# Pool inputs kept in PSUM, head sums through DRAM, token sums in groups of four: a hybrid decoder step on one core

## The chip, the core and the metric

The kernel runs on one core of a Trainium2 chip. Its engines are TensorE (PE, with its weight loads shown as PEld), VectorE (DVE), ScalarE (ACT), GpSimd (POOL) and SyncE (SP), which issues the DMAs. The metric is the device time of one execution in microseconds, the median of several runs.

## The reference

Two trunk layers of a decoder step over 576 tokens: 512 of a prompt and 8 sequences of 8 new tokens. Each layer, cut to what matters:

```python
h = rmsnorm(x, pre_g)
u, gp, q, k, v, gr = split(h @ w_in)             # 2048 -> 6 x 1024
pool_y = pool_mixer(u, ...) * silu(gp)           # window means less u, 4 groups of 256, times w_pool
ret_y = head_rmsnorm(retention(q, k, v, S0)) * silu(gr)   # 4 heads of 256
mix = concat(pool_y, ret_y) @ w_out
x = x + rmsnorm(mix, post_g)
ple = rmsnorm(p @ w_ple, ple_g)                  # 256 -> 2048
gate = sigmoid(x @ w_ple_gate + b_ple_gate)
x = x + gate * ple
```

The windows of the four pool groups are 2, 4, 8 and 16. The outputs are the tokens, the new retention states and the last 15 pool inputs of each sequence.

## The kernel before

Activations stand with channels on the 128 partitions and the 576 tokens in the free dimension, in tiles of 128 x 576 that are worked in two halves of 288 (HN). Every float32 product is made of three passes over rounded parts: `split` rounds a tensor on ScalarE (L90) and takes the rest on VectorE (L91), weights included (`split_part`, four tiles of 128 x 128 at a time).

The input projection's inner dimension of 2048 is cut in two. The first half goes through a Strassen-like scheme (`unit`, L116 to L118) and its results are stored to DRAM (`proj_dram`). The second half runs later, when the result is needed: `columns(pr)` yields the two output tiles of a pair. For each it loads the first half's result into a tile `t` of tag `part` (L478), calls `gemm` (16 channels' weights, 48 matmuls of 128 x 288, L136, into two accumulators of tag `acc`), and adds the two (L484). An accumulator is a PSUM bank; there are four of tag `acc`, two of `pb`, two of `po`.

A layer runs in this order: `in_first` (the first halves), `in_phase` (four heads, `head(0..3)`, then the pool groups 3, 2, 1, 0 with `pool_group(g)`), `out_phase` (the output projection in units, its norm, the embedding, the gate projection).

`head(h)` ends with a norm over its 256 channels (`rsqrt`, with `token_sums` at L292 and a broadcast at L310), the product with its silu gate (L653) and two stores into `m_dram[l][8 + 2h + i]`. Its state update (L354 to L377) streams 8 states through four buffers.

`pool_group(g)` loads the group's weights and state (`u` buffers, L660 and L662), and for both columns makes `e`, a tile of tag `d` with 15 zeros ahead of the prompt tokens (L668, L669), and the sample tokens behind the state in `es` (L670). GpSimd makes the window sums by doubling (L681, L682, in tiles of tag `tmp` and `es`), VectorE the mean less the input (L685 to L690). Two small gemms with the pool weights follow (L699, accumulators `po`), then the gate and scale into `y`, again of tag `d` (L703), and a store.

After each pool group, `operands(mix_loader(l, 8), [j], out_ops, tag="part")` prepares a quarter of the output projection's inputs: it loads two head outputs (tag `x`) and splits them, takes four sums and differences of their halves (`sums_of_blocks`, L194 to L197, into two tiles of tag `part`) and splits those.

In the embedding (L761 to L773) each of 16 output tiles is a gemm of 12 matmuls; ScalarE squares the two accumulators (L316, into a tile of tag `u`) and copies them (L771), TensorE adds the squares over the channels with a matrix of ones, 32 columns wide, one quarter of the tokens to each quarter of the partitions (L292, shown as two instructions per quarter), and the tile is stored.

Buffers belong to tags with a fixed count: `part` 4, `x` 4, `d` 4, `tmp` 4, `u` 6, `g` 2, `es` 2, `raw` 2 (1 MB each), `wh` and `wl` 5. The order on each engine and queue is made by a planner from the program order, the dependences and the free buffers, with costs of its own; `issue_after` and the added dependences of `after_all` constrain it by hand.

Of the kernel before, what the change touches and what calls it, by code (L numbers as in the profile page):

```python
# [38 lines left out]
def decoder_kernel(ctx: ExitStack, tc: tile.TileContext, a, decay8):  # L39
# [44 lines left out]
    ple_dram = [dram(f"ple{l}") for l in range(L)]  # L84
    gate_dram = [dram(f"gate{l}") for l in range(L)]
    proj_dram = [dram(f"proj{l}", 48) for l in range(L)]

# [40 lines left out]

    def gemm(w, xs, new=acc_tile, by_half=False):
        acc = [new()[:, :HN] for _ in range(2)]  # L130
        n = len(w)
        for hs in ((0,), (1,)) if by_half else ((0, 1),):
            for i, ((wh, wl), (xh, xl)) in enumerate(zip(w, xs)):
                for passno, (u, v) in enumerate(((wh, xh), (wh, xl), (wl, xh))):
                    for h in hs:
                        nc.tensor.matmul(  # L136
                            acc[h], u, v[:, h * HN:(h + 1) * HN],
                            start=(i == 0 and passno == 0), stop=(i == n - 1 and passno == 2),
                        )
        return acc  # L140
# [44 lines left out]

    def sums_of_blocks(ops, pairs=range(4), tag="u", engines=None):
        for j in pairs:
            x1, x2, new = ops["src"][j]
            b11, b12 = x1[:, :HN], x1[:, HN:]
            b21, b22 = x2[:, :HN], x2[:, HN:]  # L190
            eng = engines[j] if engines else nc.vector
            t12, t34 = (buf(tag) for _ in range(2))
            with order(ops):
                eng.tensor_tensor(out=t12[:, :HN], in0=b12, in1=b11, op=ALU.subtract)  # L194
                eng.tensor_tensor(out=t12[:, HN:], in0=b22, in1=t12[:, :HN], op=ALU.subtract)
                eng.tensor_tensor(out=t34[:, :HN], in0=b22, in1=b12, op=ALU.subtract)
                last = eng.tensor_tensor(out=t34[:, HN:], in0=b21, in1=t12[:, HN:], op=ALU.subtract)  # L197
            if eng is nc.vector:
                ops["tail"] = last
# [7 lines left out]
    def operands(xs, pairs=range(4), ops=None, tag="u", slots=own_slots):  # L207
        ops = operand_set() if ops is None else ops
        for j in pairs:
            blocks(xs, [j], ops, slots)  # L210
            sums_of_blocks(ops, [j], tag)
        return ops
# [77 lines left out]
    def token_sums(sums, src, start, stop):  # L290
        for q in range(4):
            nc.tensor.matmul(sums[32 * q:32 * q + 32], ones, src[:, q * QN:(q + 1) * QN], start=start, stop=stop)  # L292

    def rsqrt(out, srcs, n, sums=None):
        if sums is None:
# [11 lines left out]
        for h in range(2):  # L307
# [3 lines left out]
            nc.scalar.copy(half(out, h), rows)  # L311

    def square(out, src):
        if isinstance(src, list):
            for h in range(2):
                nc.scalar.activation(half(out, h), src[h], AF.Square)  # L316
        else:
            nc.scalar.activation(out, src, AF.Square)
# [12 lines left out]
    def load_tables():  # L331
# [8 lines left out]
        consts["invcnt"] = load_const("invcnt", [P, 4, 16])  # L340

    def after_all(ins, others):
        for other in others:
            tc.add_manual_dep(
                ins.ins, other.ins.name, mybir.DependencyInfo(mybir.DependencyClass.Sync, mybir.DependencyReason.DATA),
                reason="one burst",
            )

# [120 lines left out]
    def in_phase(l, raws, r2, rB, cos, sin):  # L469
        b_ring, st_ring, rot_ring, s0_ring = Ring(0, 12), Ring(12, 4), Ring(16, 8), Ring(24, 4)  # L470

        def columns(pr):
            keys = [("in2", p) for p in pairs] + [("out", 0, 0), ("out", 0, 1)]
            i = keys.index(("in2", pr))
            raw = raws.pop(("in2", pr))
            for c in range(2):
                t = buf("part")
                nc.sync.dma_start(out=t, in_=proj_dram[l][2 * pr + c])  # L478
                w = split_weights(raw, 8 * c, 8)
                if c == 1:  # L480
                    fetch(l, raws, keys[i + 1:i + 3])
                acc = gemm(w, r2)
                for h in range(2):
                    nc.vector.tensor_tensor(out=half(t, h), in0=acc[h], in1=half(t, h), op=ALU.add)  # L484
                yield t
# [74 lines left out]
        def head(h):  # L560
# [91 lines left out]
            for i, g in enumerate(silu_gates(20 + h)):  # L652
                nc.vector.tensor_tensor(out=o[i], in0=o[i], in1=g, op=ALU.mult)  # L653
                nc.sync.dma_start(out=m_dram[l][8 + 2 * h + i], in_=o[i])

        def pool_group(g):
# [8 lines left out]
            xs = []  # L665
            for i, t in enumerate(columns(g)):
                e = buf("d", (P, BUF + NP))
                nc.vector.memset(e[:, :BUF], 0.0)  # L668
                nc.vector.tensor_tensor(out=e[:, BUF:], in0=t[:, :NP], in1=rB[:, :NP], op=ALU.mult)  # L669
                nc.vector.tensor_tensor(  # L670
                    out=es[:, i, :, BUF:], in0=t[:, NP:].rearrange("p (b s) -> p b s", s=NS),
                    in1=rB[:, NP:].rearrange("p (b s) -> p b s", s=NS), op=ALU.mult,
# [39 lines left out]
        for j, g in enumerate(groups):  # L712
            pool_group(g)
            operands(mix_loader(l, 8), [j], out_ops, tag="part")
        return out_ops

    def mix_loader(l, first):
        def xs(k):
            t = buf("x")
            nc.sync.dma_start(out=t, in_=m_dram[l][first + k])  # L720
            return t
        return xs

    def out_phase(l, raws, ops_out):
# [5 lines left out]
        def out_step(n, g, p):  # L730
# [7 lines left out]
            if g == 0 and 1 <= p < 5:  # L738
                j = p - 1
                with order(ops[0]):  # L740
                    operands(mix_loader(l, 0), [j], ops[1], tag="d", slots=spare_slots if j < 2 else early_slots)
            if g:
# [12 lines left out]
        for k in range(2):  # L755
# [4 lines left out]
            pp.append((hi, lo))  # L760
        sums = mix_tile()[:, :QN]  # L761
        for c8 in range(2):
            raw = load_weights(a["w_ple"][l, :, c8 * 8:(c8 + 1) * 8].rearrange("p c k n -> p (c k) n"))
            w = split_weights(raw, 0, 16)
            for c in range(8):
                ct = c8 * 8 + c
                acc = gemm(w[2 * c:2 * c + 2], pp)
                t, sq = buf("part"), buf("u")
                square(sq, acc)
                for i in range(2):  # L770
                    nc.scalar.copy(half(t, i), acc[i])  # L771
                token_sums(sums, sq, ct == 0, ct == KT - 1)
                nc.sync.dma_start(out=ple_dram[l][ct], in_=t)  # L773

        def residual(first):
# [193 lines left out]
```

## Time and profile before

| | |
|---|---|
| median of 3 runs | 2217.16 us (2216.82 to 2217.84) |
| the profiled execution | 2217.77 us, span 2216.0 us |
| TensorE busy | 2185.6 us, 99% |
| weight loads busy | 2143.3 us, 97% |
| VectorE busy | 1733.7 us, 78% |
| ScalarE busy | 1057.0 us, 48% |
| GpSimd busy | 174.5 us, 8% |
| granted TensorE clock, mean | 0.996 |
| DMA | 361.99 MB, mean 163 GB/s |

The span reaches from the first to the last instruction. Matmuls overlap, so a busy TensorE is not one at its peak: where its stream is unbroken, one matmul of 128 x 288 follows another every 130 ns or so, while each is shown as 290 to 300 ns long.

### The profile page before, as it was taken

Reading aid. Unit: us, or ns where it says so; the run is one execution under the profiler, and the core shown is the slowest. Engines: PE = TensorE matmul, PEld = TensorE weight load, DVE = VectorE, ACT = ScalarE, POOL = GpSimd, SP = SyncE. Lnnn points to the kernel's source line nnn. Section 1 sums busy time; section 2 is a strip of 40 time slices with the busy share of each in tenths; the row PEclk is TensorE's granted clock in tenths of the full one; section 3 lists DMA queues with packets and bytes.
Section 4 is the critical chain, followed back from the end, with each engine's and each line's share of the span. In section 5 each row is a group of like instructions: output and inputs, shape, how many; then the busy total and the mean of one; then the engine's idle time right before and its main releaser. Section 6 shows DMA issues by size and latency. Waiting matters only on the chain.

```text
span 2216.0 us, 42622 instructions
## 1 busy us (share of the span) xinstructions
PE 2185.6 (99%) x16692; PEld 2143.3 (97%) x16692; DVE 1733.7 (78%) x3146; ACT 1057.0 (48%) x2097; POOL 174.5 (8%) x145
## 2 busy tenths in 40 slices
PE   8999999999999999999999999999999999999998
PEld 8999999999999999899999999999999899998998
DVE  8788766667689998788977886666676899988865
ACT  5465433444334555655545554434443345566532
POOL 2000000000043110000020000000002411100000
PEclk9999999999999999999999999999999999999999
DMA  6455455546443333556644444455555443345554
GB/s 222 149 195 165 155 168 165 169 157 191 154 159 129 133 128 122 196 176 208 216 157 149 169 156 152 160 177 173 164 164 165 155 135 130 106 149 192 176 194 156
DMA packets 137706, 361.99 MB, mean 163 GB/s; under 512 B 14496, under 2 KB 51872, under 8 KB 116640
## 3 DMA queue, kind: packets, MB, share of 16 engines
q1 hardware_dynamic: 137504, 359.26, 49.1%
q8 instruction: 131, 2.15, 0.4%
q14 instruction: 71, 0.58, 0.1%
HBM read 273.17 MB, written 86.04 MB: 162 GB/s over the span
## 4 chain that ended last, share of the span: by engine, by line
PE 87%; DVE 7%; DMA 4%; issue 2%; ACT 0%; SPq 0%; POOL 0%; DVEq 0%; ACTq 0%
PE acc L136 30%; PE acc L118 13%; PE acc L116 13%; PE acc L117 13%; PE acc L226 4%; PE pb L117 3%; PE pb L116 3%; PE pb L118 3%; DMA x<-ple 2%; DVE wl L91 1%; PE po L292 1%; PE po L359 1%; PE pb L375 1%; PE po L136 1%; PE pb L549 1%
## 5 line engine op out<-in xcount | busy, mean ns | idle before, releaser
L136 PE MATMUL acc<-m,wh 128*128 128x288 f32 x3584 | 661.1, 298 | 11.0 <-DVE part L484 11.0
L90 ACT CAST wh<-raw 128x512 fp32r<-128x512 f32 x567 | 350.5, 619 | 506.2 <-PE acc L136 260.7
L117 PE MATMUL acc<-m,wh 128*128 128x288 f32 x1944 | 572.8, 296 | 0.0
L116 PE MATMUL acc<-m,wh 128*128 128x288 f32 x1944 | 571.2, 295 | 0.5 <-ACT m L249 0.5
L118 PE MATMUL acc<-m,wl 128*128 128x288 f32 x1944 | 566.7, 295 | 0.7 <-DVE wl L91 0.7
L136 PEld LDWEIGHTS acc<-m,wh 128*128 128x128 f32 x3584 | 537.9, 190 | 19.1 <-issue 18.0
L91 DVE TENSOR_TENSOR wl<-raw,wh 128x512 fp32r<-128x512 f32 x567 | 407.2, 719 | 134.8 <-ACT wh L90 124.9
L136 PE MATMUL acc<-m,wl 128*128 128x288 f32 x1792 | 399.2, 296 | 0.0
L116 PEld LDWEIGHTS acc<-m,wh 128*128 128x128 f32 x1944 | 364.6, 188 | 1.9 <-ACT m L249 1.0
L117 PEld LDWEIGHTS acc<-m,wh 128*128 128x128 f32 x1944 | 364.9, 188 | 0.0
L118 PEld LDWEIGHTS acc<-m,wl 128*128 128x128 f32 x1944 | 362.4, 188 | 1.4 <-DVE wl L91 1.4
L90 ACT CAST wh<-S 128x512 fp32r<-128x512 f32 x356 | 220.4, 620 | 252.9 <-PE acc L117 139.7
L136 PEld LDWEIGHTS acc<-m,wl 128*128 128x128 f32 x1792 | 294.6, 190 | 1.9 <-issue 1.3
L91 DVE TENSOR_TENSOR wl<-S,wh 128x512 fp32r<-128x512 f32 x356 | 250.5, 705 | 22.0 <-ACT wh L90 20.5
L484 DVE TENSOR_TENSOR part<-acc,part 128x288 f32<-128x288 f32 x192 | 79.3, 449 | 62.4 <-PE acc L136 57.5
L239 POOL TENSOR_TENSOR S<-raw 128x512 f32<-128x512 f32 x45 | 70.3, 1562 | 713.6 <-DVE wl L91 352.6
L239 DVE TENSOR_TENSOR S<-raw 128x512 f32<-128x512 f32 x133 | 93.3, 701 | 8.5 <-DMA raw<-in_w_in 7.0
L682 POOL TENSOR_TENSOR es<-u 128x176 f32<-128x176 f32 x16 | 14.9, 937 | 1055.5 <-DVE u L670 1053.7
L117 PE MATMUL pb<-m,wh 128*128 128x288 f32 x324 | 95.5, 295 | 0.0
L116 PE MATMUL pb<-m,wh 128*128 128x288 f32 x324 | 95.1, 294 | 0.0
L118 PE MATMUL pb<-m,wl 128*128 128x288 f32 x324 | 95.1, 293 | 0.0
L249 ACT COPY d<-acc 128x288 f32<-128x288 f32 x228 | 86.1, 394 | 0.0
(265 smaller groups left out, 3412.1 us busy)
## 6 DMA issues: line engine op xcount, KB each, us to landing
raw<-in_w_in SPq DMA_DIRECT2D x95, 1024.0 KB, 5.3
raw<-in_w_out SPq DMA_DIRECT2D x32, 1024.0 KB, 4.9
raw<-in_w_gate SPq DMA_DIRECT2D x32, 1024.0 KB, 5.3
proj<-d SPq DMA_DIRECT2D x96, 288.0 KB, 2.1
part<-proj SPq DMA_DIRECT2D x96, 288.0 KB, 3.0
m<-in_state_ret SPq DMA_DIRECT2D x64, 256.0 KB, 3.1
out_new_ret_s<-m SPq DMA_DIRECT2D x64, 256.0 KB, 3.4
x<-m SPq DMA_DIRECT2D x48, 288.0 KB, 3.1
```

Of the source, the lines that this page charges most:

```text
L90: nc.scalar.copy(hi, src)
L91: return nc.vector.tensor_tensor(out=lo, in0=src, in1=hi.bitcast(F32), op=ALU.subtract)
L116: nc.tensor.matmul(out, wh, xh, start=start, stop=False, **kw)
L117: nc.tensor.matmul(out, wh, xl, start=False, stop=False, **kw)
L118: nc.tensor.matmul(out, wl, xh, start=False, stop=stop, **kw)
L136: nc.tensor.matmul(acc[h], u, v[:, h * HN:(h + 1) * HN], start=(i == 0 and passno == 0), stop=(i == n - 1 and passno == 2),)
L226: nc.tensor.matmul(acc[h], w[:, j], xs[h][passno == 1], start=(i == 0 and j == 0 and passno == 0), stop=(i == 1 and j == 3 and passno == 2),)
L239: eng.tensor_tensor(out=s, in0=x, in1=y, op=op)
L249: ops["tail_act"] = nc.scalar.copy(dst, src)
L292: nc.tensor.matmul(sums[32 * q:32 * q + 32], ones, src[:, q * QN:(q + 1) * QN], start=start, stop=stop)
L359: mm = nc.tensor.matmul(po_s[32 * r:32 * r + 32, bg], qrep[:, dt, b * 32:b * 32 + 32], s0s[r][:, dt], start=(dt == 0), stop=(dt == 1),)
L484: nc.vector.tensor_tensor(out=half(t, h), in0=acc[h], in1=half(t, h), op=ALU.add)
```

## The change

Three edits.

1. *Pool columns.* In `columns(pr, seeded=True)`, used by `pool_group` alone, the loaded tile `t` is copied by ScalarE into the two accumulators ahead of the gemm, whose matmuls then all accumulate (`seed`). The adds of L484 fall away there; the accumulators themselves are yielded, and the products of L669 (now two, one per half) and L670 read PSUM.
2. *Head sums.* The four sums and differences that `sums_of_blocks` takes of two head outputs are taken at the end of `head`, into two tiles of tag `x`, and stored (`sums_dram`). After a pool group they are loaded (tag `x`) instead of computed (tag `part`).
3. *Embedding squares.* The squares go to buffers of tags `tmp` (4), `g` (2) and `u` (2), and their token sums are issued four tiles at a time; the first matmul of such a burst is made to wait for the last square.

The core of the diff (`loader(tiles)` takes the place of `mix_loader(l, first)` and reads any list of DRAM tiles; `after_all` moves up unchanged):

```diff
+    sums_dram = [dram(f"sums{l}", 8) for l in range(L)]
...
-    def gemm(w, xs, new=acc_tile, by_half=False):
+    def gemm(w, xs, new=acc_tile, by_half=False, seed=None):
         acc = [new()[:, :HN] for _ in range(2)]
         n = len(w)
+        if seed is not None:
+            for h in range(2):
+                nc.scalar.copy(acc[h], half(seed, h))
...
-                            start=(i == 0 and passno == 0), stop=(i == n - 1 and passno == 2),
+                            start=(seed is None and i == 0 and passno == 0), stop=(i == n - 1 and passno == 2),
+                            skip_group_check=seed is not None,
...
+    def block_sums(eng, x1, x2, t12, t34):
+        b11, b12 = x1[:, :HN], x1[:, HN:]
+        b21, b22 = x2[:, :HN], x2[:, HN:]
+        eng.tensor_tensor(out=t12[:, :HN], in0=b12, in1=b11, op=ALU.subtract)
+        eng.tensor_tensor(out=t12[:, HN:], in0=b22, in1=t12[:, :HN], op=ALU.subtract)
+        eng.tensor_tensor(out=t34[:, :HN], in0=b22, in1=b12, op=ALU.subtract)
+        return eng.tensor_tensor(out=t34[:, HN:], in0=b21, in1=t12[:, HN:], op=ALU.subtract)
+
+    def sums_of_blocks(ops, pairs=range(4), tag="u", engines=None, sums=None):
         for j in pairs:
             x1, x2, new = ops["src"][j]
             eng = engines[j] if engines else nc.vector
+            if sums:
+                t12, t34 = sums(2 * j), sums(2 * j + 1)
+            else:
+                t12, t34 = (buf(tag) for _ in range(2))
+                with order(ops):
+                    last = block_sums(eng, x1, x2, t12, t34)
+                if eng is nc.vector:
+                    ops["tail"] = last
...
+    def together(sums, srcs, start, stop):
+        for i, src in enumerate(srcs):
+            for q in range(4):
+                mm = nc.tensor.matmul(
+                    sums[32 * q:32 * q + 32], ones, src[:, q * QN:(q + 1) * QN],
+                    start=start and i == 0, stop=stop and i == len(srcs) - 1,
+                )
+                if q == i == 0:
+                    after_all(mm, [last_square[0]])
...
-                nc.scalar.activation(half(out, h), src[h], AF.Square)
+                last_square[0] = nc.scalar.activation(half(out, h), src[h], AF.Square)
...
-        def columns(pr):
+        def columns(pr, seeded=False):
...
+                if seeded:
+                    yield gemm(w, r2, seed=t)
+                    continue
                 acc = gemm(w, r2)
...
+            sums = [buf("x") for _ in range(2)]
+            block_sums(nc.vector, *o, *sums)
+            for i, t in enumerate(sums):
+                nc.sync.dma_start(out=sums_dram[l][2 * h + i], in_=t)
...
-            for i, t in enumerate(columns(g)):
+            for i, acc in enumerate(columns(g, seeded=True)):
                 e = buf("d", (P, BUF + NP))
                 nc.vector.memset(e[:, :BUF], 0.0)
-                nc.vector.tensor_tensor(out=e[:, BUF:], in0=t[:, :NP], in1=rB[:, :NP], op=ALU.mult)
+                nc.vector.tensor_tensor(out=e[:, BUF:BUF + HN], in0=acc[0], in1=rB[:, :HN], op=ALU.mult)
+                nc.vector.tensor_tensor(out=e[:, BUF + HN:], in0=acc[1][:, :NP - HN], in1=rB[:, HN:NP], op=ALU.mult)
                 nc.vector.tensor_tensor(
-                    out=es[:, i, :, BUF:], in0=t[:, NP:].rearrange("p (b s) -> p b s", s=NS),
+                    out=es[:, i, :, BUF:], in0=acc[1][:, NP - HN:].rearrange("p (b s) -> p b s", s=NS),
                     in1=rB[:, NP:].rearrange("p (b s) -> p b s", s=NS), op=ALU.mult,
                 )
...
             pool_group(g)
-            operands(mix_loader(l, 8), [j], out_ops, tag="part")
+            operands(loader(m_dram[l][8:]), [j], out_ops, sums=loader(sums_dram[l]))
...
+        squares = []
         for c8 in range(2):
...
-                t, sq = buf("part"), buf("u")
+                t, sq = buf("part"), buf(("tmp", "tmp", "tmp", "tmp", "g", "g", "u", "u")[ct % 8])
                 square(sq, acc)
                 for i in range(2):
                     nc.scalar.copy(half(t, i), acc[i])
-                token_sums(sums, sq, ct == 0, ct == KT - 1)
                 nc.sync.dma_start(out=ple_dram[l][ct], in_=t)
+                squares.append(sq)
+                if len(squares) == 4:
+                    together(sums, squares, ct == 3, ct == KT - 1)
+                    squares = []
```

## Rows read from the trace of the kernel before

**Rows 1.** The page: TensorE's own line (busy time, share of the span, instructions) and the engines' shares of the chain that ended last.

```profile
PE 2185.6 (99%) x16692; PEld 2143.3 (97%) x16692; DVE 1733.7 (78%) x3146; ACT 1057.0 (48%) x2097; POOL 174.5 (8%) x145
...
PE 87%; DVE 7%; DMA 4%; issue 2%; ACT 0%; SPq 0%; POOL 0%; DVEq 0%; ACTq 0%
```

**Rows 2.** The waits of TensorE, longest first in total: who waited, for whom, us in total, times, longest.

```profile
PE acc L136 <- DVE part L484: 11.0, 4, 3.0
```

**Rows 3.** Windows around the waits of rows 2, TensorE alone. Columns: stretch in us, its length, TensorE busy (matmuls), granted clock, DMA share, GB/s.

```profile
640.00:643.00 3.00, 0.07 (x1) 0.83 0.97 303
643.00:646.00 3.00, 2.92 (x12) 0.50 0.97 368
646.00:649.00 3.00, 3.00 (x15) 0.53 0.87 307
...
1741.00:1744.00 3.00, 3.00 (x13) 0.52 0.86 310
...
1774.00:1777.00 3.00, 3.00 (x18) 0.71 0.28 65
1777.00:1780.00 3.00, 3.00 (x19) 0.73 0.95 383
```

**Rows 4.** The time order of VectorE in the pool stage of layer 0: start in us, length in us, instruction; in brackets the idle time before it and who ended it.

```profile
570.26 0.81 DVE L484 TENSOR_TENSOR part<-acc,part 128x288 f32<-128x288 f32 x2
...
576.77 0.82 DVE L484 TENSOR_TENSOR part<-acc,part 128x288 f32<-128x288 f32 x2 [2.01 <-PE acc L136]
...
585.97 0.35 DVE L670 TENSOR_TENSOR u<-part,long 128x64 f32<-128x64 f32 x2
...
600.09 0.81 DVE L484 TENSOR_TENSOR part<-acc,part 128x288 f32<-128x288 f32 x2
...
613.57 0.44 DVE L484 TENSOR_TENSOR part<-acc,part 128x288 f32<-128x288 f32 x1
...
633.80 0.95 DVE L703 SCALAR_TENSOR_TENSOR d<-po,c_pool_scale,g 128x288 f32<-128x288 f32 x2
634.26 0.07 DVE L668 MEMSET d<- 128x15 f32 x1
634.67 1.29 DVE L669 TENSOR_TENSOR d<-part,long 128x512 f32<-128x512 f32 x2
...
638.89 0.35 DVE L670 TENSOR_TENSOR u<-part,long 128x64 f32<-128x64 f32 x2
...
642.50 0.81 DVE L484 TENSOR_TENSOR part<-acc,part 128x288 f32<-128x288 f32 x2
...
665.48 1.29 DVE L669 TENSOR_TENSOR d<-part,long 128x512 f32<-128x512 f32 x2
```

**Rows 5.** The time order of SP's queue in the same stage (start, length of the issue, DMA).

```profile
578.67 0.38 SPq L662 DMA_DIRECT2D u<-in_state_pool  x1
...
639.13 0.80 SPq L478 DMA_DIRECT2D part<-proj  x2
```

**Rows 6.** The chain in order of time: start, length, piece. One unbroken stretch of accumulator matmuls.

```profile
288.83 30.37 PE acc L136 x233
```

**Rows 7.** DMA issues by line: count, KB of one, median us from issue to landing.

```profile
u<-in_state_pool SPq DMA_DIRECT2D x8, 184.0 KB, 2.8
```

**Rows 8.** The time order of the engines on the tail of head 3 of layer 0: state product, token sums, row broadcast (TensorE), window sums (GpSimd), pooled value (VectorE).

```profile
583.68 1.07 PE L359 MATMUL po<-m,u 128*32 128x256 f32 x16
...
598.39 0.70 PE L292 MATMUL po<-tmp,ones 128*32 128x144 f32 x16
...
608.59 1.14 PE L310 MATMUL po<-tmp,pick 128*128 128x144 f32 x8
609.87 3.17 POOL L681 TENSOR_TENSOR tmp<-tmp 128x520 f32<-128x520 f32 x2 [8.65 <-PE po L310]
...
625.26 0.66 DVE L687 SCALAR_TENSOR_TENSOR tmp<-tmp,d 128x496 f32<-128x496 f32 x1
```

**Rows 9.** Groups of instructions by line: count | busy us, mean ns of one | idle time of the engine before them.

```profile
L249 ACT COPY d<-acc 128x288 f32<-128x288 f32 x228 | 86.1, 394 | 0.0
...
L316 ACT ACTIVATE u<-acc 128x288 f32<-128x288 f32 x64 | 26.2, 417 | 8.5 <-PE acc L136 7.1
L771 ACT COPY part<-acc 128x288 f32<-128x288 f32 x64 | 25.4, 406 | 0.0
...
L292 PE MATMUL po<-u,ones 128*32 128x144 f32 x256 | 18.8, 294 | 0.0
...
L196 DVE TENSOR_TENSOR part<-x 128x288 f32<-128x288 f32 x8 | 7.6, 948 | 0.0
```

**Rows 10.** The time order of TensorE in the embedding stage of layer 0: bursts of token sums (line 292) and the matmuls around the shortest of them.

```profile
883.35 0.70 PE L292 MATMUL po<-tmp,ones 128*32 128x144 f32 x16
...
891.61 1.92 PE L292 MATMUL po<-u,ones 128*32 128x144 f32 x56
...
898.27 0.43 PE L136 MATMUL acc<-d,wh 128*128 128x288 f32 x2
898.63 0.44 PE L292 MATMUL po<-u,ones 128*32 128x144 f32 x4
899.00 0.40 PE L136 MATMUL acc<-d,wl 128*128 128x288 f32 x1
```

**Rows 11.** A window of the same stage. Columns: stretch, length, busy time (instructions) of TensorE, weight loads, VectorE, ScalarE, GpSimd, then granted clock, DMA share, GB/s.

```profile
892.00:916.00 24.00, 24.00 (x222) 18.32 (x212) 19.87 (x32) 20.16 (x57) 0.00 (x0) 1.00 0.79 269
```

More of the change, by code (lines that the diff above doesn't have):

```diff
@@ L184, in blocks @@
         return ops
-    def sums_of_blocks(ops, pairs=range(4), tag="u", engines=None):
+    def block_sums(eng, x1, x2, t12, t34):
[6 more added lines that the diff above has]
+    def sums_of_blocks(ops, pairs=range(4), tag="u", engines=None, sums=None):
         for j in pairs:
             x1, x2, new = ops["src"][j]
-            b11, b12 = x1[:, :HN], x1[:, HN:]
-            b21, b22 = x2[:, :HN], x2[:, HN:]
             eng = engines[j] if engines else nc.vector
[L192 to L199, printed above, removed]
+            if sums:
[6 more added lines that the diff above has]
+                    ops["tail"] = last
             for src, n1, n2 in ((t12, "t1", "t2"), (t34, "t3", "t4")):
@@ L205, in sums_of_blocks, with operands @@
         return ops
-    def operands(xs, pairs=range(4), ops=None, tag="u", slots=own_slots):
+    def operands(xs, pairs=range(4), ops=None, tag="u", slots=own_slots, sums=None):
         ops = operand_set() if ops is None else ops
@@ L210, in operands @@
             blocks(xs, [j], ops, slots)
-            sums_of_blocks(ops, [j], tag)
+            sums_of_blocks(ops, [j], tag, sums=sums)
         return ops
@@ L311, in rsqrt, with after_all @@
             nc.scalar.copy(half(out, h), rows)
+    last_square = [None]
+    def after_all(ins, others):
+        for other in others:
+            tc.add_manual_dep(
+                ins.ins, other.ins.name, mybir.DependencyInfo(mybir.DependencyClass.Sync, mybir.DependencyReason.DATA),
+                reason="one burst",
+            )
     def square(out, src):
@@ L340, in load_tables @@
         consts["invcnt"] = load_const("invcnt", [P, 4, 16])
[L342 to L347, printed above, removed]
     def retention_state(l, h, s0_ring, qrep, kst, vst, po_s):
@@ L713, in in_phase, with loader @@
             pool_group(g)
-            operands(mix_loader(l, 8), [j], out_ops, tag="part")
+            operands(loader(m_dram[l][8:]), [j], out_ops, sums=loader(sums_dram[l]))
         return out_ops
-    def mix_loader(l, first):
+    def loader(tiles):
         def xs(k):
             t = buf("x")
-            nc.sync.dma_start(out=t, in_=m_dram[l][first + k])
+            nc.sync.dma_start(out=t, in_=tiles[k])
             return t
@@ L740, in out_step @@
                 with order(ops[0]):
-                    operands(mix_loader(l, 0), [j], ops[1], tag="d", slots=spare_slots if j < 2 else early_slots)
+                    operands(loader(m_dram[l]), [j], ops[1], tag="d", slots=spare_slots if j < 2 else early_slots)
             if g:
```

## The prediction, made before the changed kernel was run

> **What bounds the kernel now.** The page comes first, for the shares [rows 1]: TensorE is busy 99% of the span and 87% of the chain, so a microsecond counts only where TensorE gets or loses one. Next come TensorE's waits [rows 2]: nearly everything it waits for is one thing, four waits of 11.0 us in all for the add of line 484, which empties the accumulators. Then the windows around them, one row per stretch [rows 3]: in 640:643 TensorE does nothing, and behind it, as behind the wait at 1738 in layer 1, the granted clock is at half (0.50 to 0.53, the 1.2 GHz level), with 12, 15 and 13 matmuls in 3 us where 130 ns apiece would give 23; of the shorter pair of waits only layer 1's costs clock (18 and 19 matmuls). So a wait of 3 us costs itself and up to as much again. Last the time order of VectorE and the queues in the pool stage of layer 0 [rows 4, 5], where the reader should see why that add is late. Layer 1 repeats layer 0 1098 us later, so I count one layer and double it.
>
> In those rows u0 and u1 of group 3 are added at 570.26 and 576.77, their sample tokens multiplied at 585.97. Group 2's are added by 600.09 and 613.57, but their products (line 669) come at 634.67, and the sample ones (line 670) at 638.89. For 25 to 39 us they sit in `part`, and the next two loads into `part` go out at 639.13, just behind. So the add of 642.50 is late, and TensorE stands. Why are the products late? The memset of `e` (634.26) lies between the two halves of the second `y` of group 3 (second one from 633.80). The same order returns in the later groups. Tiles of one tag are handed out in program order: `e` of a group can't exist before the last `y` of the group ahead has been given its buffer. This reading carries the forecast.
>
> **The change, part by part.** *Adds removed.* 16 pool columns lose two adds each: 32 x 0.44 us [rows 4] = 14.1 us of VectorE; 16 more products come back. `part` is no longer held, so the four waits go: 11.0 / 2 = 5.5 us a layer. The clock behind them: against 23 matmuls per 3 us the windows of [rows 3] miss 11 + 8 + 10 + 5 + 4 = 38, at 130 ns (233 in 30.37 us, [rows 6]) 4.9 us, 2.5 a layer. Gain 8.0 us a layer.
>
> *PSUM held instead.* Now a pool column stays in its two accumulators until its three products are through. There are four accumulators, two columns' worth, handed out in order too. So the third column after a u0 cannot start before u0 is read, and that read waits for `e` (after the last `y`) and for the pool state's load.
>
> Group 3: u1 is ready at 576.8 [rows 4]. TensorE then went straight on; now it waits for the product of line 670. Its load is issued at 578.67 [rows 5] and takes 2.8 us [rows 7], so 581.5 at the earliest; the product stood at 585.97. I take 585: 8.2 us, less some 1.5 us of state matmuls (583.68, [rows 8]) that run in it: 6.7. Bounds 4.7 and 8.0.
>
> Group 2: from 585 TensorE has four columns (g0, g1 of group 3, u0, u1 of group 2). One is 48 x 130 ns = 6.3 us; 25 us together. Between 576.8 and 613.6 at the latest it did the same four columns and some other work; I reckon 8.5 us of it, 7.0 after the 1.5. So it runs dry at 585 + 25 + 7 = 617. When is u0 of group 2 read? After the second `y` of group 3, whose chain is head 3's tail [rows 8]: state product 583.68, sums 598.39, row broadcast 608.59, GpSimd from 609.87 (it waits for the buffer that the broadcast frees), pooled value 625.26, second `y` 633.80. From 583.68 to 598.39 there are 14.7 us for about 6 us of work, since TensorE's queue puts columns between; from 625.26 to 633.80 8.5 us for about 4.5. With the columns gone these stretches can shrink by 8 and 4 us, and the first state product may come 1.4 us earlier: 620 at the earliest. As ordered now it is 638.89. I take 625, nearer the low end, since TensorE stands idle in exactly the places where columns were filled in. 8 us, less the 3.2 us of the pool weights' 24 matmuls, which move into the gap: 4.8. Bounds 0 and 18.7.
>
> Two new idle stretches are as long as or longer than those of [rows 3], so the clock pays: 1.5 us a window of 3 us, 3.0 a layer (0 to 6). Later groups: from one release to the next TensorE has four columns and 3.2 us, 28.4 us; the chain (GpSimd, split, weights, `y`, load) took 30.8 us from 634.67 to the next such product (665.48 [rows 4]) with columns filled in, so I add nothing.
>
> *Seeds.* 32 ScalarE copies of about 394 ns (the same shape out of PSUM [rows 9]; none into PSUM is in the trace). ScalarE is 48% busy, so they are covered, except that each column's two copies sit between the emptying of its banks and its first matmul. If the emptying is late, 0.8 us shows. Behind a waiting copy on ScalarE stand the weight casts, and TensorE behind those. I take 1.0 a layer, 0 to 3.
>
> *Sums as heads end.* Four subtractions a head (up to 948 ns [rows 9], at most 3.8 us together) move from the pool stage to the head's end. 8 stores and 8 loads of 288 KB a layer join SP's queue; they are issued behind the head's `m` stores and in the group's loads of `x`, and weight loads stand behind them. Their sizes are those of the stores and loads beside them. VectorE is 78% busy and the heads show no TensorE wait for it. I count nothing; without that cover head 3's own sums stand before group 3's pooled values, up to 3.8 us on the chain above (inside its bounds). The tag `x` is handed out in order too, so group 3's loads now follow head 3's sums, still far ahead of the output projection.
>
> *Squares in fours.* Around a burst of 4 the matmul before ends at 898.70 and the one behind at 899.40 [rows 10]: 0.70 where one matmul takes 0.13, so a burst costs 0.57. A burst of 16 lasts 0.26 longer (0.70 against 0.44), so 0.83, and 40 instructions more 1.22 (0.70 to 1.92), 0.24 per square of 8. A layer has 128 such instructions: 56, 8 and sixteen times 4 in the time order (256 in both layers [rows 9]), that is 1.92 + 0.58 + 9.1 = 11.6 us. Four bursts of 32 cost 4 x 1.32 = 5.3. TensorE gains 6.3. Against it: seven squares were finished at 891.61 (the 56), from `u`. The first four now come from `tmp`, in order behind the two last squares and the work tile of the root, which is held until its broadcast ends just before 891. Some three tiles fewer are then done by 891: 3 x 1.58 = 4.7 us for TensorE, 3 x 1.65 for ScalarE (417 and 406 ns, two each [rows 9]), which was busy 20.2 of 24 us in 892:916 [rows 11] and would need 25.1. ScalarE takes over as the limit. I take 0, bounds -5 and +5.
>
> The Trainium skill ("TensorE: Matmul & The Clock Gate", section "Measured speedup vs the span model") says that matmuls packed side by side span one matmul plus about 4 ns per further tile. By it a burst costs nothing beyond its columns, joining saves nothing, and ScalarE's bill remains: +5 a layer. The rows' 0.57 us speaks against it; the columns of four in a burst do run side by side, as it says.
>
> *Sum, a layer:* 6.7 + 4.8 + 3.0 - 8.0 + 1.0 + 0 = +7.5; two layers +15.0. On the profiled execution's 2217.77 us (span 2216.0 and 1.8 around it) 2232.8; the median lies 0.6 lower: **2232.2 us**.
>
> **The rivals.** A difference under 0.2% (4.4 us) is about what a measurement of this kernel can't tell from none.
> - *PSUM is let go in time (faster).* It decides at one point: whether group 3's second `y` comes before TensorE runs dry at 617. VectorE's lighter load (14.1 us fewer, and the subtractions gone from the stage) speaks for it; the in-order handing out speaks against. If neither wait exists: -8.0 and -3 for the squares, -11.0 a layer, 2195; if the first stays in part, 2200 to 2212. Chance 0.34.
> - *The two sides cancel.* No second gap, first gap 6.7 and 1.5 of clock against 8.0: 2217. Chance 0.11.
> - *The order of today stays (slower still).* `e` at 634.67 and its load at 638.89: 6.7 + 18.7 + 4 - 8.0 + 1 = +22 a layer, 2261. The order in [rows 4] is for it, TensorE's emptier queue against. Chance 0.12.
> - *Joined bursts save nothing*, the rule above: +12.5 a layer, 2242. Chance 0.03. The rule of evacuating early ("PSUM — Partial Sum Buffer", section "Summary: rules for kernel authors", the Trainium skill) points the way of the forecast.
>
> **How the numbers follow.** The forecast has 0.40. Slower: 0.40 + 0.12 + 0.03 = 0.55; same 0.11; faster 0.34. All bounds at their best give 2200 with the first gap and 2190 without, at their worst (8.0 + 18.7 + 6 - 8.0 + 3 + 5 a layer) 2282. Leaving out about 0.08 below and 0.10 above gives 2196 to 2256; the forecast's own range is 2222 to 2248.
>
> **What would show it.** Right: no TensorE wait for line 484 in the pool stage; instead an idle stretch near 577 to 585 and one near 617 to 625, both ended by a ScalarE seed or a VectorE product, the clock at half behind them, and both again 1098 us later; `e` of a group still behind the last `y` of the group ahead; bursts of 32 and ScalarE nearly full around 890 to 920. Wrong: TensorE continuous from 570 to 690, or `e` products that follow their columns within a few microseconds; or a shorter embedding stage with ScalarE still idle in it.

## The result and the profile after

The changed kernel takes **2232.28 us** (median of four runs, 2230.53 to 2233.35) against 2216.99 for the kernel before, timed beside it: a ratio of 1.007, 95% interval 1.0054 to 1.0086, slower by 15.3 us. The profiled execution took 2231.92 us, its span is 2230.1 us.

The page of the kernel after, the two lines that answer to [rows 1]:

```profile
PE 2176.3 (98%) x16692; PEld 2142.0 (96%) x16692; DVE 1725.1 (77%) x3130; ACT 1070.5 (48%) x2129; POOL 163.9 (7%) x145
...
PE 88%; DMA 5%; DVE 4%; issue 1%; ACT 1%; SPq 0%; POOL 0%; DVEq 0%; ACTq 0%; POOLq 0%
```

TensorE is busy 9 us less in a span 14 us longer, so it stands still more. Where, its waits tell (who waited, for whom, us in total, times, longest; the whole kernel after):

```profile
PE po L142 <- ACT u L91: 26.7, 6, 9.9
...
PE po L310 <- ACT tmp L348: 2.2, 2, 1.1
PE acc L142 <- DVE d L701: 2.2, 2, 1.3
...
PE acc L142 <- ACT acc L137: 0.6, 1, 0.6
```

The 11.0 us of [rows 2] are gone: no row names the add any more (it is line 512 now). In their place stands a new one, 26.7 us in six times: the small products with the pool weights (tile `po`) wait until ScalarE has rounded the pooled value (L91). The time order of TensorE around the first of them, layer 0:

```profile
610.56 0.42 PE L142 MATMUL acc<-m,wl 128*128 128x288 f32 x2
620.90 0.85 PE L142 MATMUL po<-u 128*128 128x288 f32 x2 [9.91 <-ACT u L91]
...
624.93 2.12 PE L142 MATMUL po<-u 128*128 128x288 f32 x6 [1.30 <-ACT u L91]
627.42 2.87 PE L142 MATMUL po<-u 128*128 128x288 f32 x12 [0.37 <-DVE d L736]
631.61 0.54 PE L142 MATMUL acc<-m,wh 128*128 128x288 f32 x2 [1.32 <-DVE d L701]
```

The last column of group 2's input ends at 610.98, the next column begins at 631.61: 20.6 us without one. Of those, 24 matmuls at some 130 ns, about 3.2 us, are work; 17.4 us are lost. The last row says what ends it: the product of line 701, which reads group 2's first column out of PSUM. The list names the pooled value because that wait stood first in TensorE's queue; the stop as a whole belongs to the accumulators, as the runs with more buffers for `e` bear out below. VectorE in time order says why line 701 is late:

```profile
570.64 0.45 DVE L701 TENSOR_TENSOR d<-acc,long 128x288 f32<-128x288 f32 x1
...
577.74 0.46 DVE L701 TENSOR_TENSOR d<-acc,long 128x288 f32<-128x288 f32 x1 [2.45 <-PE acc L142]
...
587.26 0.35 DVE L703 TENSOR_TENSOR u<-acc,long 128x64 f32<-128x64 f32 x2
...
618.16 0.66 DVE L720 SCALAR_TENSOR_TENSOR tmp<-tmp,d 128x496 f32<-128x496 f32 x1
...
623.42 0.66 DVE L720 SCALAR_TENSOR_TENSOR tmp<-tmp,d 128x496 f32<-128x496 f32 x1
...
630.67 0.51 DVE L736 SCALAR_TENSOR_TENSOR d<-po,c_pool_scale,g 128x288 f32<-128x288 f32 x1
631.12 0.44 DVE L701 TENSOR_TENSOR d<-acc,long 128x288 f32<-128x288 f32 x1
631.13 0.07 DVE L700 MEMSET d<- 128x15 f32 x1
...
633.60 0.50 DVE L736 SCALAR_TENSOR_TENSOR d<-po,c_pool_scale,g 128x288 f32<-128x288 f32 x1
```

Group 3's two columns are read at 570.64 and 577.74, as they end. Group 3's two pooled values follow at 618.16 and 623.42 (line 720, one for each column). Group 2's columns stand ready from 602 and 611 and are read at 631.12: between the first half (630.67) and the second half (633.60) of group 3's second `y`, exactly as the memset of `e` lay between the halves in [rows 4]. The windows of TensorE through the stop (stretch, length, busy, granted clock, DMA share, GB/s):

```profile
611.00:620.50 9.50, 0.00 (x0) 0.77 0.94 307
620.50:624.00 3.50, 2.18 (x6) 0.50 0.48 156
...
628.00:631.50 3.50, 2.29 (x12) 0.76 0.92 294
631.50:635.00 3.50, 3.39 (x25) 1.00 0.87 265
```

The granted clock falls while TensorE stands (0.77 in the first row) and is at half (0.50, the 1.2 GHz level) while most of the 24 matmuls of the pool weights trickle; when the columns begin again it is full.

For the rest of the kernel the two traces can be laid over each other, since both hold 16692 matmuls: the end of the n-th matmul (counted from 0) in each, in us, at the borders of the stages.

```
matmul   before    after   after - before
 4448     591.1    591.8    +0.7
 5282     710.6    720.9   +10.3   pool stage of layer 0 behind
 6533     877.3    887.1    +9.9
 6950     925.5    932.6    +7.0   embedding of layer 0 behind
12788    1688.7   1697.4    +8.7
13622    1809.0   1827.7   +18.7   pool stage of layer 1 behind
14873    1975.6   1994.0   +18.4
15290    2023.8   2038.7   +14.8   embedding of layer 1 behind
16680    2208.6   2222.8   +14.2
```

The pool stage loses 9.6 and 10.0 us, the embedding gains 2.9 and 3.6, and 1.1 us in all drift elsewhere.

### The profile page after: what moved, and what is told of

The parts are those of the page before. It is cut to its first block, busy times and chain, and to the rows that moved or that the text cites. A ratio compares the mean times of both kernels' runs of the same rounds, so it can differ in the third digit from the quotient of the medians.

```text
span 2230.1 us, 42710 instructions
## 1 busy us (share of the span) xinstructions
PE 2176.3 (98%) x16692; PEld 2142.0 (96%) x16692; DVE 1725.1 (77%) x3130; ACT 1070.5 (48%) x2129; POOL 163.9 (7%) x145
## 4 chain that ended last, share of the span: by engine, by line
PE 88%; DMA 5%; DVE 4%; issue 1%; ACT 1%; SPq 0%; POOL 0%; DVEq 0%; ACTq 0%; POOLq 0%
PE acc L142 31%; PE acc L118 13%; PE acc L117 13%; PE acc L119 13%; PE acc L239 4%; PE pb L118 3%; PE pb L117 3%; PE pb L119 3%; DMA x<-ple 2%; DMA out_new_ret_s<-m 1%; PE po L142 1%; DMA x<-m 1%; PE po L384 1%; DVE m L92 1%; PE pb L400 1%
## 5 line engine op out<-in xcount | busy, mean ns | idle before, releaser
L91 ACT CAST wh<-raw 128x512 fp32r<-128x512 f32 x567 | 350.8, 620 | 547.2 <-PE acc L142 288.9
L91 ACT CAST wh<-S 128x512 fp32r<-128x512 f32 x356 | 220.9, 620 | 242.0 <-PE acc L118 142.7
L512 DVE TENSOR_TENSOR part<-acc,part 128x288 f32<-128x288 f32 x160 | 66.2, 451 | 71.7 <-PE acc L142 71.1
```

The lines of the kernel that those rows point to most:

```text
L91: nc.scalar.copy(hi, src)
```

## The experiments

The kernel before was run again beside each group of them; its median there was 2217.04, 2217.06, 2217.27 and 2216.55.

**One edit at a time.** Three kernels, each the kernel before with one of the three edits. In the first, 2 and 3 are undone, in the second 1 and 3, in the third 1 and 2, for instance

```diff
-            operands(loader(m_dram[l][8:]), [j], out_ops, sums=loader(sums_dram[l]))
+            operands(loader(m_dram[l][8:]), [j], out_ops, tag="part")
```

> The kernel before with the first edit alone (pool columns seeded and read in PSUM); sums of blocks and embedding squares as before. Theory: this edit makes the whole loss, since the pool stage's stop of TensorE (610.98 to 631.61 us of layer 0 after the change) comes from accumulators held until `e` is handed out. Lined up by matmul number the pool stage lost 9.4 us in layer 0 and 9.2 in layer 1 and the embedding gained 3.2 a layer, so without the embedding's gain 2217 + 19 to 21 = 2236 to 2238 us. Rival: the sums taken at the end of head 3 (four subtractions of VectorE between 613.56 and 619.12) hold back the first pooled values by their 2.3 us a layer and the same again in clock; then without them the loss is 4 to 9 us smaller: 2227 to 2233.

> The kernel before with the second edit alone (sums of two head outputs taken as the head ends, stored, and loaded after a pool group). Theory: nothing on TensorE's path; the four waits for the add of line 484 stay, since `part` is still held by pool columns: 2217, within 4 us either way. Rival: the subtractions left `part` (two tiles less in its ring), so the loads into `part` go out earlier and some of the 11.0 us of waits fall: 2206 to 2212. Rival on the other side: the subtractions stand before group 3's pooled values, 2.3 us a layer: 2221 to 2224.

> The kernel before with the third edit alone (embedding squares in bursts of four tiles). Theory: lined up by matmul number the embedding gained 2.8 us in layer 0 and 3.6 in layer 1, 6.4 together: 2210.6. Rival: that gain is the first part of a shift that is given back elsewhere (1.8 us were lost between the two embeddings): 2213 to 2217. Rival by the prediction's even sum: ScalarE eats the gain, 2217.

Measured: seeding alone 2248.53 us (1.0142, 1.0125 to 1.0158), sums alone 2229.75 (1.0055, 1.0041 to 1.0069), squares alone **2209.35 (0.9964, 0.9951 to 0.9978)**. The squares came out as the laid-over traces said, 7.7 us faster. The other two missed both theory and rivals on the slow side, and the parts did not add up: +31.5, +12.7 and -7.7 make 36.5, the change 15.3. Something slow was in both single edits and not in the change. TensorE's waits of the first edit alone show it:

```profile
PE po L142 <- ACT u L91: 23.8, 4, 9.9
PE po L384 <- DMA m<-in_state_ret: 6.4, 3, 4.6
```

The stop is there (first row), and beside it TensorE waits for the loads of head 3's states. SP's queue there:

```profile
574.50 1.11 SPq L379 DMA_DIRECT2D m<-in_state_ret  x2
575.70 0.42 SPq L103 DMA_DIRECT2D raw<-in_w_in  x1
576.21 0.90 SPq L402 DMA_DIRECT2D out_new_ret_s<-m  x2
585.11 1.06 SPq L379 DMA_DIRECT2D m<-in_state_ret  x2
```

and in the changed kernel:

```profile
573.89 1.02 SPq L402 DMA_DIRECT2D out_new_ret_s<-m  x2
575.32 0.35 SPq L103 DMA_DIRECT2D raw<-in_w_in  x1
576.95 1.24 SPq L379 DMA_DIRECT2D m<-in_state_ret  x2
```

The last two state loads reuse the tiles that the two stores (line 402) empty. With a 1 MB weight load issued 0.5 us ahead of the stores, the loads go out 8.9 us behind them; with the stores ahead of it, 3.1 us. The planner had turned the order around in both single edits (in the second edit 574.22, 574.73 and 583.82). That is no part of any edit, so it was put back. In every other run of this document the two stores stand ahead of the load, in both layers.

**The order on SP held.** The same two kernels with one weight load queued behind the stores:

```diff
+                if key == ("in2", 6):
+                    with tc.issue_after(first_stores[0].ins):
+                        raws[key] = load_weights(ap)
+                else:
+                    raws[key] = load_weights(ap)
```

(`first_stores` holds the last store of the first four states; everything behind it in the code stands seven lines later, so the add of line 512 is line 519 here.)

> The first edit alone again (2248.5 us), with one weight load of SP's queue put behind the two stores of head 3's new states, as before and after the change have it; in the first edit alone the planner had put it ahead of them (1 MB at 575.70, stores at 576.21, and the next two state loads, which need the stored tiles, at 585.11 instead of 576.95). Theory: that swap is by itself worth the shift at the state products, lined up by matmul number 7.1 us in layer 0 and 5.9 in layer 1, so 2248.5 - 13 = 2235.5, and the seeding itself costs 18.5. Rival: the state loads come late for a reason that seeding brings along (longer use of the tiles, the DMA engines' load), and the order on SP changes nothing: 2245 to 2249.

> The second edit alone again (2229.8 us), with the same weight load of SP's queue put behind the two state stores. Theory: the swap cost 4.9 us in layer 0 and 2.2 in layer 1, so 2222.6, which leaves about 5.6 us for the sums themselves (four subtractions ahead of group 3's pooled values). Rival: the swap is harmless here, and the sums cost all of it: 2228 to 2231.

Measured: 2235.39 (1.0084, 1.007 to 1.0098) and 2221.51 (1.002, 1.0011 to 1.0029). Both theories hold within about 1 us: the order of three DMAs was worth 13.1 and 8.2 us. Now the parts add up: seeding +18.3, sums +4.5, squares -7.7, together +15.1 against 15.3 measured. Each of the three is known to some 2 to 3 us either way, so that they meet within tenths is chance. With the sums alone, TensorE's waits are now

```profile
PE acc L142 <- DVE part L519: 10.7, 2, 5.5
...
PE po L142 <- ACT u L91: 4.2, 4, 1.8
```

where [rows 2] had four waits of 3.0 at most for the add, and the kernel before waited 1.0 us in two for the pooled value: the add is waited for in fewer and longer pieces, the pooled value longer. That fits subtractions that stand ahead of group 3's pooled values; that they make the whole 4.5 us is not shown.

**Buffers for `e`.** First two buffers of its own, in the changed kernel:

```diff
-                e = buf("d", (P, BUF + NP))
+                e = buf("e", (P, BUF + NP))
```

> The changed kernel with `e` in a tag of its own (two buffers) instead of `d`, so that a group's `e` needn't wait for the last `y` of the group ahead. Theory: the first bank of a column is then let go as soon as the column is through, the second still waits for its state tile, which is the next use of a buffer that holds group 3's pool weights. So TensorE gets the first halves of two more columns, 48 matmuls or 6.3 us, in the stop at 611: 2232.3 less 2 x 6.3 and up to 2 us of clock, 2217 to 2220. Rival: the stop is the pool weights' own matmuls waiting in TensorE's queue for group 3's pooled value, whatever is free behind them: 2232 as before, with a stop of about 10 us that ends near 621.

Measured: 2231.9 us (1.0068, 1.0053 to 1.0083), as the changed kernel. The time is the rival's, the cause is not: the pool weights' products no longer head the list of waits.

```profile
PE acc L142 <- DVE e L701: 19.4, 2, 9.7
PE acc L142 <- ACT acc L137: 9.5, 2, 5.4
```

TensorE now waits for the product itself, which VectorE does at 620.81, straight behind the last reader of group 3's first `e` (line 719, 619.73 to 620.75). Two buffers are one group's worth: `e` of group 2 had moved from behind the second `y` to behind the pooled value, which frees the buffer. My theory had counted one cause where a second lay right behind it. So `d` was given to `e` alone in this stage, four buffers, by writing `y` over its gate:

```diff
-                y = buf("d")
+                y = gate
```

> The changed kernel with `y` written over its gate, so that tag `d` is used by `e` alone in the pool stage, four buffers, two groups' worth. Theory: `e` of group 2 was late because a buffer of its own was missing, either behind the second `y` (the change) or behind the pooled value that frees group 3's `e` (own tag of two buffers). With two groups' worth the products that read group 2's columns follow at about 604 and 611 instead of 631, two of four accumulators come free there, and one column after another runs through those two: the stop of 20 us at 611 goes or shrinks below 5 us, in both layers. Of the 20 us that the pool stage loses per layer some 5 stay: 2232 - 2 x 12 to 16 = 2200 to 2208. Rival: the products are held by the state tile (sample product) as much as by `e`: the stop only moves by 5 to 6 us, 2220 to 2232. Rival: the next stop takes its place, since gates now wait for stores of `y`: 2215 to 2230.

Measured: 2218.15 us (1.0009, 0.9999 to 1.0019): 14.1 us gained, half of the 24 to 32 that the theory gave. VectorE reads group 2's columns at 601.01 and 613.83, and the stop of 20.6 us is gone. What TensorE still waits for at the pool columns, in both layers:

```profile
PE acc L142 <- DVE u L703: 8.0, 2, 4.0
...
PE acc L142 <- DVE d L701: 3.5, 2, 1.8
PE acc L142 <- ACT acc L137: 3.4, 4, 1.5
```

So the stop was `e`'s missing buffer. The longest wait is now for the sample products (line 703, 645.80 in layer 0): their state tile is loaded at 638.83, as group 3's last products with the pool weights end (638.91), whose operands lie in `u` too. The next experiment gave it a place:

```diff
-            es = buf("u", (P, 2, NB, SEG))
+            es = buf("st", (P, 2, NB, SEG))
```

> As the run before (`y` over its gate), and the pool state in a tag of its own with two buffers instead of the six of `u`, where it stood behind group 3's weights and values. Theory: the sample products come early too, all four accumulators are free, and little more is gained, since two accumulators were enough: within 4 us of the run before. Rival: two accumulators leave TensorE waiting for each add, and four take off another 5 to 10 us.

Measured: 2216.1 us (0.9996, 0.9988 to 1.0005), 2 us under the run before. No wait for an accumulator of a pool column is left. Instead:

```profile
PE po L142 <- ACT u L91: 9.0, 7, 1.8
```

The pool weights' products come later still (group 3's last twelve at 641.73, against 627.42 in the changed kernel) and now stand between columns that could run.

**Was the stop's length a sum of two gaps?** I had predicted a first gap at 577 to 585, and there is none. To force it, both accumulators of a pool column were held until the pool state is there:

```diff
+                nc.vector.tensor_tensor(out=es[:, i, 0, BUF:], in0=acc[0][:, :NS], in1=rB[:, :NS], op=ALU.mult)
                 nc.vector.tensor_tensor(
                     out=es[:, i, :, BUF:], in0=acc[1]...
```

> The changed kernel with one small product more per pool column, which reads the first accumulator of the column together with the sample product (its values are overwritten by the sample product behind it), so that both accumulators are held until the pool state is there. Theory: the gap of 577 to 585 that was predicted is not there because the first accumulators of two columns, let go at 571 and 578, take one whole column half by half; held, the gap comes, 7 to 9 us up to 586 or 587 in layer 0 and the same in layer 1. But the end of the stop at 631 is set by head 3's tail and not by TensorE's work, so the stop from 611 gets shorter by as much: 2230 to 2238 in all. Rival: the two gaps add up, 2 x 8 us more: 2246 to 2250. Rival: no gap at 577, since the sample products come at once: 2232 with the stop as it was.

Measured: 2241.59 us (1.0114, 1.0097 to 1.0131), between the theory and the rival. Windows of TensorE:

```profile
577.50:584.00 6.50, 0.00 (x0) 0.82 0.79 276
584.00:590.00 6.00, 4.73 (x27) 0.50 0.38 125
...
625.00:637.20 12.20, 2.39 (x17) 0.82 0.99 353
637.20:641.00 3.80, 3.80 (x16) 0.50 0.48 152
```

The gap comes where it was predicted, though longer: no column from 577.5 to 590.2. (The list of waits puts 6.7 us of it down to the loads of head 3's state, because the state product heads TensorE's queue; it runs at 584.17, as in the changed kernel at 584.00, so those loads are no later than there.) And the second stop is shorter: it begins at 624.8 instead of 611.0 and ends at 637.2. That it ends later than 631.6 is the edit's own doing, since the first accumulator is now held for the state too (samples at 636.96). In the main the two gaps trade against each other, as the theory had it, but 4.7 us a layer are left that it had not counted; I put them down to half the clock behind both stops and the later end, without having parted the two.

**Without seeding.** The third edit with `y` over its gate, then the same with seeding (and the order on SP held), then the first with the pool state in a tag of its own:

```diff
-            for i, acc in enumerate(columns(g, seeded=True)):
+            for i, t in enumerate(columns(g)):
...
-                y = buf("d")
+                y = gate
```

> The third edit alone (2209.4 us) with `y` written over its gate; pool columns added in `part` and sums taken in the pool stage, as before the change. Theory: the wait for a buffer for `e` was what made the adds of line 484 late in the kernel before, too; with two groups' worth of `d` for `e` those four waits of 11.0 us go, with the half clock behind them about 4.9 more: 2209.4 - 11 to 16 = 2193 to 2198. Rival: the adds wait for `part` through the sample products, whose state tile stands behind the group ahead: half of it at most, 2201 to 2206. Rival: the gates, now held until `y` is stored, hold `part` instead: 2207 to 2212.

> As the run before, with the first edit (seeding) added again, sums of blocks still taken in the pool stage, and the weight load of SP behind head 3's state stores, as in the kernel before. It tells what seeding is worth once `e` has its buffers. Theory: nothing or a small loss, since accumulators are then held by the sample products (one wait of 4 us a layer was left in the changed kernel with `y` over its gate): 2 to 10 us over the run before. Rival: VectorE's 32 adds fewer pay now: 2 to 8 us under the run before.

> The third edit with `y` over its gate (2209.2 us) and the pool state in a tag of its own, two buffers. Theory: the two waits of 4.0 and 3.4 us for the add of line 512 that are left there come from the sample products, whose state tile stands behind group 3's weights in `u`; with the state early they go, with up to 1 us of half clock each: 2209.2 - 7 to 9 = 2200 to 2202. Rival: as in the changed kernel with the same two edits, other waits take their place (pool weights' matmuls waiting for the pooled values, 6 to 8 us in all): 2207 to 2212.

Measured: **2209.2** (0.9964, 0.9951 to 0.9977), 2209.3 (0.9967, 0.9954 to 0.998) and 2214.49 us (0.9988, 0.9979 to 0.9997). The first theory fell. The products of `e` did move, to 603.49 in layer 0 instead of 634.67, but the waits for the add only went from 11.3 us in four (third edit alone) to

```profile
PE acc L142 <- DVE part L512: 7.4, 2, 4.0
```

and the time did not change: the sample product (641.42) held `part` as long as before. Seeding on top is worth nothing either way once `e` has its buffers. With the state early as well, the add is hardly waited for (0.5 us once), and the pooled values are:

```profile
PE po L142 <- ACT u L91: 12.4, 6, 3.2
```

That kernel is 5 us slower than the other two. With each buffer that is moved out of the way TensorE meets the chain from head 3's tail through group 3's pooled values in another place; no run here shortened that chain itself. The three fastest kernels (the third edit alone, with `y` over its gate, and with seeding on top; 2209.2 to 2209.35 us) beat the kernel before by 0.3 to 0.4% and the changed one by 1.0%.

## Why the prediction was right, and where it was not

The forecast was 2232.2 us and the time is 2232.28. The mechanism was the predicted one: accumulators held until `e` is handed out behind the second `y`. But the sum came out through terms that missed in both directions: that it met the time within 0.1 us is luck, the direction and the cause of the loss are not.

- *The four waits of line 484* (-5.5 - 2.5 a layer): right. No such wait is left.
- *First gap, 6.7*: did not come. I took a column as one thing that needs both accumulators of group 3's first column. It runs as two halves: the products of 570.64 and 577.74 let go one accumulator of each column, and the next column took those two, first one half, then the other; VectorE adds its halves one at a time (584.11 and 586.29) where two came together before. Only the second accumulators waited for the sample product (587.26, where 585 was taken; its state's load took 5.4 us, where [rows 7] had 2.8). Where both are held, the gap is there (above). VectorE's first such add, and TensorE's window of the stretch, in the changed kernel:

```profile
584.11 0.46 DVE L512 TENSOR_TENSOR part<-acc,part 128x288 f32<-128x288 f32 x1 [0.33 <-PE acc L142]
```

```profile
577.60:585.60 8.00, 8.00 (x69) 1.00 0.65 241
```

- *Second gap, 4.8*: 17.4. It began at 611 and not at 617, because the first gap was missing (617 less 6.7 is 610.3), and ended at 631.6 and not at 625. I had let 14.7 us of head 3's tail shrink by up to 8, and the way from a pooled value to the second `y` from 8.5 to 4.5. State product to token sums went from 14.7 to 13.1 us only (584.00 to 597.08). The 625.26 of [rows 8] is group 3's second pooled value, not its first; like with like, the first came 1.2 us earlier (618.16) and the second 1.8 (623.42). From the second to the second `y` it took 7.2 us: the last twelve matmuls with the pool weights ran mostly at half the clock, and the `y` stood in VectorE's queue behind a split of the output projection's operands (to 630.75). So the second `y` came 3.1 us earlier, not 9. The first pooled value and those twelve matmuls in the kernel before (2.87 us for the twelve after it):

```profile
619.38 0.66 DVE L687 SCALAR_TENSOR_TENSOR tmp<-tmp,d 128x496 f32<-128x496 f32 x1
```

```profile
631.82 1.75 PE L136 MATMUL po<-u 128*128 128x288 f32 x12
```

  What came to 11.5 us for both gaps was 17.4 in one.
- *Clock, 3.0*: nothing behind the long stop, where the columns began at full clock. It fell on the pool weights' matmuls instead: the twelve above took 1.1 us longer, on the way to the second `y` and so inside the 17.4. In layer 1 a second stop (1749.1 to 1752.2) was followed by 13 matmuls in 3 us at 0.61, some 1.3 us.
- *Seeds, 1.0*: 0.6 us in one wait of the whole kernel.
- *Sums, nothing*: 2.2 a layer by the run with the order on SP held, inside the bound of 3.8; the waits fit the chain that it named.
- *Squares, 0, as 6.3 less ScalarE's bill*: -2.9 and -3.6. TensorE's side was right. (By its own rule the bursts of 56 and 8 cost 2.05 and 0.66 us, not 1.92 and 0.58, which makes the gain 6.5 and not 6.3.) A joined burst, in TensorE's time order:

```profile
907.56 0.29 PE L142 MATMUL acc<-d,wl 128*128 128x288 f32 x1
907.78 0.70 PE L310 MATMUL po<-g,ones 128*32 128x144 f32 x16
908.30 0.67 PE L310 MATMUL po<-u,ones 128*32 128x144 f32 x16
908.90 0.54 PE L142 MATMUL acc<-d,wh 128*128 128x288 f32 x2
```

From the end of the matmul before (907.85) to the end of the second one behind (909.44) 1.59 us, less 0.26 for those two: 1.33 for 32 instructions, where 1.32 was reckoned from [rows 10]. ScalarE's bill was too high; the window answers to [rows 11]:

```profile
892.00:916.00 24.00, 22.70 (x226) 21.69 (x230) 20.63 (x39) 20.82 (x62) 0.00 (x0) 1.00 0.61 203
```

ScalarE is busy 20.8 of 24 us, not full. What it costs are single waits of TensorE: 1.1 us for the last square of the first burst, 1.2 in two ahead of columns in layer 0 and 0.9 in one in layer 1. They make most of the 3.4 and 2.7 by which the gain falls short of 6.3; where the rest went is open. The Trainium skill ("TensorE: Matmul & The Clock Gate", section "Measured speedup vs the span model") has no term for entering and leaving a burst of packed matmuls, by which joining would have saved nothing; the 0.57 us of a burst of four [rows 10] and 7.7 us in the run of this edit alone say otherwise.

In the pool stage the terms make 17.4 + 0.3 - 8.0 = 9.7 in layer 0, against 9.6 from the laid-over traces and 7.5 predicted. That it closes so well is chance too: with the second stop and its clock the same sum makes 17.2 + 3.1 + 1.3 - 8.0 = 13.6 in layer 1, against 10.0. Both leave out shorter waits on either side, which I have not added up. In the seeded kernel the sums have no share of their own there that I could separate. Of the rivals, "PSUM is let go in time" named the right point, whether the second `y` comes before TensorE runs dry; it came 20 us after. In this point the rival "the order of today stays" was nearest: the order survived nearly unchanged (products at 631.12 instead of 634.67), and its second gap of 18.7 is closer to 17.4 than my 4.8. Its 2261 came out too high mostly by the first gap and the clock, which did not come.

The reading behind the forecast was only half right about the kernel before: there the adds were late for the sample product and its state tile at least as much as for `e`. Giving `e` its buffers took 3.9 of 11.3 us of waits and none of the time.

## What to carry to other kernels

When a result stays in PSUM, ask for every single bank which instruction reads it last and what that instruction needs besides, a buffer above all. Here the gaps in front of one late release were in the main one gap with one end, and a stall on a long chain moved when what waited behind it was freed. Before parts of a change are compared one by one, compare the order of instructions on each queue: here a planner's swap of three DMAs, no part of any edit, was worth as much as an edit.

## What the runs showed of the hardware that I had not expected

*A load in front of a store on one queue.* Two 256 KB stores issued 0.5 us behind a 1 MB load took 8.9 us from issue to landing, where they took 3.1 issued ahead of it (DMA issues of the stretch: how many, KB, median us to landing; first the first edit alone, then the changed kernel):

```profile
raw<-in_w_in SPq DMA_DIRECT2D x1, 1024.0 KB, 8.6
out_new_ret_s<-m SPq DMA_DIRECT2D x2, 256.0 KB, 8.9
```

```profile
out_new_ret_s<-m SPq DMA_DIRECT2D x2, 256.0 KB, 3.1
```

The Trainium skill ("DMA: Bandwidth & Descriptors", section "Queues, rings and completion order") says that SP has one ring on each DMA engine, that descriptors are consumed in ring order, and that completions need not come in that order. The trace agrees with the ring order: the two stores behind the load landed 0.8 us after it (576.21 + 8.9 against 575.70 + 8.6). Turning the three around gave 13.1 us back in one kernel and 8.2 in another.

*A ScalarE copy into PSUM* took 0.40 us for 128 x 288 (32 copies of 392 to 404 ns in the changed kernel), as out of PSUM (394 ns, [rows 9]); no row of the kernel before had shown that.
